# Four directly multiplied tiles of an up-projection: another place for one result half, two more PSUM banks, and a later point in each slot for low parts and eviction adds

## The chip, the cores and the metric

One Trainium2 chip, and one of its cores. The metric is the device time of one execution in microseconds (us), the median of several runs. Engines are named as the profile names them: PE (TensorE), DVE (VectorE), ACT (ScalarE), POOL (GpSimd) and SP, whose queue issues the DMAs of this stage.

## The reference

One decoder layer on x of 1 x 1024 x 1024: three attention and convolution branches behind one input projection, one output projection, and a gated MLP with a causal convolution. The change lies where the output projection ends and the MLP begins:

```python
x = x + jnp.einsum('bsd,de->bse', y, w_o[l])
h2 = rmsnorm(x, ln2_g[l])
u = jnp.einsum('bsd,df->bsf', h2, w_up[l])                # 1024 -> 2 * 2816
u = causal_dwconv(u, ffn_conv_w[l], ffn_conv_b[l])        # 3 taps along s
hidden = jax.nn.silu(u[..., :D_FF]) * u[..., D_FF:]
x = x + jnp.einsum('bsf,fd->bsd', hidden, w_down[l])
```

Everything is float32; the kernel must come close to that.

## The kernel before

Everything is kept transposed: features on the 128 partitions, the 1024 positions along the free axis in two halves of 512. A float32 product is made of three float32r matmuls (`mm3`): weight high part by input high part, by input low part, and weight low part by input high part. A weight block of 128 x 512 is loaded by SP, ACT casts it to its high part (`whs`, L856), and POOL or DVE subtracts to get the low part (`wls`, L857): that is `wsplit`.

The up-projection has 22 tiles j, each with a gate half and a value half of 128 features. Tiles 4 to 20 are made by a scheme with seven products for each tile (`pipeline`, banks `mA`, `m`). It needs sums and differences of the input's quarters, which don't exist yet when the MLP begins. So the first four tiles are multiplied directly, in `spread`, while those are being made. `spread` is a list of 40 slots, each of 12 matmuls on one weight block: slots 0 to 7 ("o") are the second half of the output projection, slots 8 to 39 are (j, i, q): tile j, positions half i, and q = 0 to 3 for gate and value (q % 2) with the input's first or second 512 features (q // 2).

Names of the input quarters: b11 and b21 are the first positions half (first and second 512 features), b12 and b22 the second, and t1 = b12 - b11. In half i = 0, q < 2 multiplies b11 into banks p0 and p1 of the tile, and q = 2, 3 multiplies b21 into p2 and p3; the result is p2 + p0 (gate) and p3 + p1 (value). In half i = 1, q < 2 adds the product of t1 onto what p0 and p1 still hold, which makes it that of b12, and q = 2, 3 adds that of b22. So those matmuls may only start when the first half's eviction has read p0 and p1. An eviction (`slot_evict`) is an ACT copy of one bank into `ur` and, for i = 0, a DVE add of the other.

The order on DVE, ACT and POOL is the order in which `spread` calls them: for slot s the matmuls, the eviction of slot s - 1, the split of the weights of slot s + 3, then `work`, which takes jobs from `jobs_` by a budget of units: `scaled` and `comb_split` make b, t1, t2, t3, t4 (a DVE operation, an ACT cast for the high part, and a DVE subtraction for the low part one call later), and `conv_value`, `conv_gate`, `conv_end` are the causal convolution of finished tiles (an ACT operation, two DVE taps of 1023 and 1022 columns, Silu on ACT, a DVE product of 1024). PE's own order is made by a scheduler. The evictions in `LATE` (slots 15, 34, 35) are put off: that of slot 15 because the tile `rb`, into which the value half of j = 1 goes, still holds a norm, and those of 34 and 35 because both `ur` buffers still hold tile 2 until its convolution is done.

Ahead of `spread`, `out(e, 1, 0)` makes a first part of the output projection's second half, with two PSUM buffers of tag "mm" (`mm_ps`); `pt_ps` is a tag with five.

Of the kernel before, what the change touches and what calls it, by code (L numbers as in the profile page):

```python
# [8 lines left out]
F32 = mybir.dt.float32  # L9
# [51 lines left out]
def hybrid_trunk(ctx: ExitStack, tc: tile.TileContext, xT, par, win, wvf, wo, wup, wdn,  # L61
# [96 lines left out]
    with ExitStack() as cb_:  # L158
# [19 lines left out]
        def mm_ps(name):  # L178
            return ps1.tile([P, HALF], F32, tag="mm", name=name, bufs=2)
# [455 lines left out]
        def out(e, i, part):  # L635

            if part == 0:
                if e % 2 == 0:
                    xh_[i].append(pair_tile(f"x1_{i}_{e}", [P, 2, HALF], F32))
                nc.sync.dma_start(X(e, i), xT[e][:, HS[i]])  # L640
            w = load_w(wo[e][:, 4 * part:4 * part + 4], 4, f"wo{e}_{i}_{part}")
            ps = mm_ps(f"oc{e}_{i}_{part}")
            yield from mm_gen(ps, w, y_part(part, i), slice(0, HALF))
            V.tensor_add(X(e, i), ps, X(e, i))

# [131 lines left out]
    def ur_tile(name, shape=None):  # L777
        return fp.tile(shape or [P, S], F32, tag="ur", name=name, bufs=2)
# [68 lines left out]

    wcount = [0]

    def wsplit(j, n, t, nk=4, eng=G):  # L850
        with tc.high_priority():
            wcount[0] += 1
            pool, tag, b = (fp, "x", 1) if wcount[0] % 4 == 0 else (wp, "", 3)
            hi = pool.tile([P, 4, P], F32R, tag=f"{tag}wh", name=f"wh{j}_{n}", bufs=b)[:, 0:nk]
            lo = pool.tile([P, 4, P], F32R, tag=f"{tag}wl", name=f"wl{j}_{n}", bufs=b)[:, 0:nk]
            A.copy(hi, t)  # L856
            eng.tensor_sub(lo, t, hi.bitcast(F32))  # L857
        return [(hi[:, k, :], lo[:, k, :]) for k in range(nk)]

    def prod(ps, n, w, x=None, first=True, **kw):  # L860
# [280 lines left out]

    HT = ((0, 0), (1, 0), (0, 1), (1, 1), (2, 0), (2, 1), (3, 0), (3, 1))
    slots = [("o", e, 0) for e in range(DT)] + [(j, i, q) for j, i in HT for q in range(4)]
    pro = pipeline(NFF - 1)

    LATE = [slots.index(s) for s in ((1, 0, 3), (3, 0, 2), (3, 0, 3))]
    raws, ws_, ps_, gone = {}, {}, {}, set()
    acc2 = r2b[:, HS[1]]
    g1 = [half_pair(f"g1_{k}", "c") for k in range(4)]
# [7 lines left out]
        nc.sync.dma_start(raws[s], src)  # L1157

    def slot_prep(s):
        ws_[s] = wsplit("s", s, raws.pop(s), eng=G if s < 11 else V)  # L1160

    def slot_mm(s):
        j, i, q = slots[s]
        w = ws_.pop(s)
        if j == "o":
            ps_[s] = bank(f"o{i}")
            prod(ps_[s], 0, w, x=y_last)
        elif i == 0:
            ps_[j, q] = bank(f"p{j}_{q}")
            prod(ps_[j, q], 1 if q < 2 else 2, w, skip_group_check=True)  # L1170
        else:
            prod(ps_[j, q % 2], 5 if q < 2 else 3, w, first=False, skip_group_check=True)

    def slot_evict(s):

        j, i, q = slots[s]
        gone.add(s)
        if j == "o":
            x = X(i, 1)
            V.tensor_add(x, ps_[s], x)  # L1180
            A.activation(acc2 if i == 0 else r2vt[:, 1] if i == DT - 1 else sq2[:, i % 2], x, AF.Square)
            return 1
        if q < 2:
            return 0
        if (i, q) == (0, 2):
            ur[j] = [cp.tile([P, S], F32, tag=t, name=f"ur{j}{t}", bufs=1) for t in ("rb2", "rb")] if j == 1 else                 [ur_tile(f"ur{j}_{c}") for c in range(2)]
        u = ur[j][q - 2][:, HS[i]]
        if i == 0:
            A.copy(u, ps_[j, q])
            V.tensor_add(u, ps_[j, q - 2], u)  # L1190
            return 1
        A.copy(u, ps_[j, q - 2])
        return 0
# [4 lines left out]
    def jobs_():  # L1198

        for r, b in enumerate((b11, b21)):  # L1200
            for k in range(4):
                def f(r=r, b=b, k=k):
                    scaled(b[k], 4 * r + k, 0)
                    comb_split(("b11", "b21")[r], k, b[k])
                yield 0, 2, f

        def norm():
            ps = bank("r2ps1")
            colsum(ps, acc2, r2vt[:, 1, :])
            rsqrt(r2b[:, HS[1]], ps, D, r2vt[:, 0, :], r2vt[:, 1, :])  # L1210
        yield 9, 4, norm
        yield 0, 1, comb_low
        for k in range(4):
            def f(k=k):
                scaled(b12[k], k, 1)
                V.tensor_sub(b12[k], b12[k], b11[k])
                comb_split("t1", k, b12[k])
            yield 0, 3, f
        for k in range(4):
            def f(k=k):  # L1220
                scaled(b22[k], 4 + k, 1)
                if k == 3:
                    slot_evict(LATE[0])
                comb_split("b22", k, b22[k])
            yield 0 if k < 3 else LATE[0] + 1, 2, f

        def combos(k):
            V.tensor_sub(b22[k], b22[k], b12[k])
            comb_split("t2", k, b22[k])
            yield 2  # L1230
            V.tensor_sub(b11[k], b22[k], b11[k])
            comb_split("t3", k, b11[k])
            yield 2
            V.tensor_sub(b21[k], b22[k], b21[k])
            comb_split("t4", k, b21[k])
            yield 2

        def conv_value(j):
            gated[j] = [None, cv_tile(j)]
            conv_first(j, ur[j][1], gated[j][1], 1)  # L1240
            yield 0
            for d in (1, 2):
                conv_tap(j, ur[j][1], gated[j][1], 1, d)
                yield 2

        def conv_gate(j):
            cg = gated[j][0] = x_tile(f"cg{j}").rearrange("p i s -> p (i s)")
            conv_first(j, ur[j][0], cg, 0)
            yield 0
            for d in (1, 2):  # L1250
                conv_tap(j, ur[j][0], cg, 0, d)
                yield 2
            A.activation(cg, cg, AF.Silu)
            yield 0

        def conv_end(j):
            comb_low()
            cg, cv = gated[j]
            V.tensor_mul(cv, cv, cg)
            tail[j] = store(j)  # L1260
            yield 2

        def turns(*gens):
            gens = list(gens)
            while gens:
                for g in list(gens):
                    u = next(g, None)
                    if u is None:
                        gens.remove(g)
                    else:  # L1270
                        yield u

        def stored(j):
            for f in tail[j]:
                f()
                yield 2

        def late():
            for s in LATE[1:]:
                slot_evict(s)  # L1280
                yield 1


        for first, gens in ((0, [combos(0)]), (0, [combos(1)]), (21, [conv_value(0), combos(2)]),
                            (0, [conv_gate(0), combos(3)]), (24, [conv_value(1), conv_end(0)]),
                            (24, [conv_gate(1)]), (25, [conv_end(1)]), (0, [stored(1)]), (32, [conv_value(2)]),
                            (32, [conv_gate(2)]), (34, [conv_end(2)]), (35, [late()]), (35, [pro_steps()])):
            gen = turns(*gens)
            while True:
                got = []  # L1290
                def f(gen=gen, got=got):
                    got.append(next(gen, None))
                    return got[0]
                yield first, None, f
                if got[0] is None:
                    break
# [6 lines left out]
    def spread():  # L1303
# [4 lines left out]
        for s in range(FRONT):  # L1308
            slot_prep(s)
            slot_load(s + FRONT)  # L1310
        units = 0

        def work(units):
# [6 lines left out]

        for s in range(len(slots)):
            units = min(units, 2) + 4
            if slots[s][0] == 3 and slots[s][1]:
                while LATE[-1] not in gone:
                    work(1)
            slot_mm(s)
            if s and s - 1 not in LATE:
                units -= slot_evict(s - 1)
            if 3 <= s < 2 + DT - 1:
                V.tensor_add(acc2, acc2, sq2[:, (s - 2) % 2])  # L1330
                units -= 1
            n = s + FRONT
            if n < len(slots):
                slot_prep(n)
                units -= n >= 11
                if n + FRONT < len(slots):
                    slot_load(n + FRONT)
            else:
                units = work(99)
                assert job is None  # L1340
                next(pro)
            units = work(units)
        assert job is None
        slot_evict(len(slots) - 1)
        after(FIRST - 1, 0)
        drain(pro)

# [169 lines left out]
```

## Time and profile before

| | |
|---|---|
| time of 3 runs, median (lowest to highest) | 1292.29 us (1291.47 to 1294.94) |
| the profiled execution | 1292.03 us, of it 1290.2 us from first to last instruction |
| PE busy | 1212.5 us, 94% |
| DVE, ACT, POOL busy | 1004.1, 635.1, 452.5 us |
| granted TensorE clock, mean | 0.979 of full speed |

All times below are from the start of that span. Each matmul row on PE gives 0.39 us, since matmuls overlap; at full clock they start 0.227 us apart, so a slot of 12 takes 2.72 us. Idle time of DVE, ACT and POOL only matters where PE waits for its end.

### The profile page before, as it was taken

The page shows a single profiled execution, that of the slowest core. Times are in us where ns is not written, and L with a number is a line of the kernel's source. Part 1 is how long each engine was busy: PE and PEld are TensorE (multiplying, and loading weights), DVE is VectorE, ACT ScalarE, POOL GpSimd, SP SyncE. Part 2 cuts the span into 40 slices and gives each one's busy share as a digit, 9 for nine tenths or more (in the row PEclk, how much of TensorE's full clock was granted, in tenths as well). Part 3 has the DMA queues.
Part 4 walks back from the last instruction along what each step waited for, and adds up shares of the span by engine and source line. Part 5 has one row for each costly group of instructions (what it writes and reads, how often), then busy time and mean ns, then how long its engine had stood idle before and what let it go on. Part 6 is the DMA issues. An engine that isn't in the chain of part 4 may idle for free.

```text
span 1290.2 us, 17279 instructions
## 1 busy us (share of the span) xinstructions
PE 1212.5 (94%) x6061; PEld 986.0 (76%) x6061; DVE 1004.1 (78%) x1521; ACT 635.1 (49%) x1158; POOL 452.5 (35%) x361
## 2 busy tenths in 40 slices
PE   7999899999999998999988999999999989999996
PEld 5897577777777876777666888888888868786795
DVE  8799886654565577777786888888888898979756
ACT  6422365564556475544564554554544564443233
POOL 4575122322242141341001121111112476867754
PEclk9899799999999999999998999999999989999998
DMA  6102021111001233232231332332233364634203
GB/s 221 42 17 68 23 67 33 58 58 58 25 26 42 76 106 115 71 125 82 82 131 58 106 116 105 106 121 69 98 122 118 128 192 150 195 109 141 74 24 131
DMA packets 64758, 118.93 MB, mean 92 GB/s; under 512 B 6800, under 2 KB 26784, under 8 KB 64672
## 3 DMA queue, kind: packets, MB, share of 16 engines
q1 hardware_dynamic: 64096, 117.57, 27.5%
q8 instruction: 47, 0.77, 0.3%
q14 instruction: 39, 0.32, 0.1%
q10 hardware_dynamic: 576, 0.28, 0.1%
HBM read 93.89 MB, written 23.93 MB: 91 GB/s over the span
## 4 chain that ended last, share of the span: by engine, by line
PE 48%; DVE 7%; issue 3%; ACT 2%; POOL 2%; DMA 1%; DVEq 0%; SPq 0%; POOLq 0%; ACTq 0%
PE mA L116 5%; PE mA L117 5%; PE mA L118 5%; PE m L116 4%; PE m L118 4%; PE m L117 4%; PE d L118 3%; PE d L117 3%; PE d L116 3%; POOL wld L857 1%; PE oc L116 1%; PE oc L117 1%; PE oc L118 1%; PE dl L117 1%; PE dl L116 1%
## 5 line engine op out<-in xcount | busy, mean ns | idle before, releaser
L857 POOL TENSOR_TENSOR wl<-a,wh 128x512 fp32r<-128x512 f32 x38 | 51.2, 1349 | 277.2 <-ACT wh L856 275.1
L453 DVE TENSOR_TENSOR pl<-pt,ph 128x512 fp32r<-128x512 f32 (+1 forms) x120 | 75.3, 635 | 59.3 <-ACT ph L452 56.2
L118 PE MATMUL d<-hc,wld 128*128 128x512 f32 x252 | 100.8, 401 | 8.2 <-POOL wld L857 8.0
L117 PE MATMUL d<-hc,whd 128*128 128x512 f32 x252 | 99.8, 396 | 1.9 <-DVE hc L1132 1.9
L116 PE MATMUL d<-hc,whd 128*128 128x512 f32 x252 | 99.5, 396 | 0.8 <-ACT hc L1131 0.4
L418 ACT ACTIVATE w<-w,mn 128x128 f32<-128x128 f32 (+7 forms) x96 | 73.8, 770 | 49.5 <-DVE mn L412 49.1
L273 DVE SCALAR_TENSOR_TENSOR yc<-gv,prm,yc 128x1023 f32<-128x1023 f32 (+29 forms) x60 | 86.1, 1435 | 0.9
L452 ACT CAST ph<-pt 128x512 fp32r<-128x512 f32 (+1 forms) x120 | 63.5, 538 | 41.1 <-PE pt L448 30.1
L463 PE MATMUL av<-ph,VS 128*128 128x256 f32 x240 | 64.6, 288 | 10.6 <-ACT ph L452 6.8
L448 PE MATMUL pt<-idf,w 128*128 128x128 f32 x432 | 69.7, 280 | 4.2 <-ACT w L418 3.4
L857 POOL TENSOR_TENSOR wld<-a_d,whd 128x384 fp32r<-128x384 f32 x48 | 61.0, 1275 | 16.2 <-ACT whd L856 13.4
L118 PEld LDWEIGHTS d<-hc,wld 128*128 128x128 f32 x252 | 48.1, 191 | 23.4 <-POOL wld L857 13.7
L856 ACT CAST wh<-a 128x512 fp32r<-128x512 f32 x72 | 44.8, 622 | 38.4 <-issue 23.7
L857 DVE TENSOR_TENSOR wl<-s,wh 128x512 fp32r<-128x512 f32 x51 | 40.9, 802 | 28.4 <-ACT wh L856 28.4
L464 PE MATMUL av<-pl,VS 128*128 128x256 f32 x240 | 62.0, 291 | 0.9 <-DVE pl L453 0.9
L463 PEld LDWEIGHTS av<-ph,VS 128*128 128x128 f32 x240 | 45.8, 191 | 21.6 <-ACT ph L452 10.4
L448 PEld LDWEIGHTS pt<-idf,w 128*128 128x128 f32 x432 | 50.1, 142 | 12.1 <-ACT w L418 5.0
L116 PE MATMUL m<-t,wh 128*128 128x512 f32 x152 | 59.1, 389 | 0.0
L117 PE MATMUL m<-t,wh 128*128 128x512 f32 x152 | 59.1, 389 | 0.0
L118 PE MATMUL m<-t,wl 128*128 128x512 f32 x152 | 59.1, 389 | 0.0
L117 PEld LDWEIGHTS d<-hc,whd 128*128 128x128 f32 x252 | 47.9, 190 | 12.7 <-DVE hc L1132 2.7
L103 POOL TENSOR_TENSOR wl_wo<-raw_wo,wh_wo 128x512 fp32r<-128x512 f32 x24 | 32.2, 1344 | 72.1 <-ACT wh_wo L102 65.5
(418 smaller groups left out, 3965.0 us busy)
## 6 DMA issues: line engine op xcount, KB each, us to landing
a<-in_wup SPq DMA_DIRECT2D x72, 256.0 KB, 2.5
tr<-td SPq DMA_DIRECT2D x27, 512.0 KB, 5.0
a_d<-in_wdn SPq DMA_DIRECT2D x48, 192.0 KB, 2.4
d<-in_wup SPq DMA_DIRECT2D x32, 256.0 KB, 2.5
raw_wo<-in_wo SPq DMA_DIRECT2D x24, 256.0 KB, 2.6
td<-cv SPq DMA_DIRECT2D x9, 512.0 KB, 2.8
td<-ta SPq DMA_DIRECT2D x9, 512.0 KB, 3.8
td<-tb SPq DMA_DIRECT2D x9, 512.0 KB
```

The source lines that it names most:

```text
L116: T.matmul(ps, lhsT=wh, rhs=xh[:, sl], start=first, stop=False, **kw)
L117: T.matmul(ps, lhsT=wh, rhs=xl[:, sl], start=False, stop=False, **kw)
L118: T.matmul(ps, lhsT=wl, rhs=xh[:, sl], start=False, stop=last, **kw)
L273: V.scalar_tensor_tensor(y[:, d:], u[:, 0:S - d], col(wc + 30 - d), y[:, d:], op0=ALU.mult, op1=ALU.add)
L418: A.activation(w[:, 0:nk], w[:, 0:nk], AF.Exp, scale=-1.0, bias=mn[h], accum_out=den[qi // 4][:, 4 * h + qi % 4:4 * h + qi % 4 + 1])
L448: T.transpose(pt[:, P * b:P * b + P], ws[2 * i + j, h][:, P * kt:P * kt + P], idf)
L452: A.copy(ph[:, 0:w], pt[:, 0:w])
L453: V.tensor_sub(pl[:, 0:w], pt[:, 0:w], ph[:, 0:w].bitcast(F32))
L463: T.matmul(o, lhsT=vt, rhs=phl[0][:, r], start=kt == 0, stop=False)
L464: T.matmul(o, lhsT=vt, rhs=phl[1][:, r], start=False, stop=kt == 2 * i + 1)
L856: A.copy(hi, t)
L857: eng.tensor_sub(lo, t, hi.bitcast(F32))
```

## The change

It does five things. (1) The value half of tile 1 goes into a buffer of tag "cb" of the MLP's pool and not into `rb`, so the eviction of slot 15 is no longer put off, and `combos(3)` (t2, t3, t4 of the last chunk) moves behind the first tile's convolution. (2) Slots 18 to 21 change places in pairs: t1 products of tiles 0 and 1 come first, then the b22 products. (3) The t1 products of tile 3 start new banks p4 and p5; its second half is evicted as copy and add, two adds more on DVE. (4) Low parts of the weights and eviction adds are put in a list `later` and issued at the end of the slot, behind `work`. (5) `out(e, 1, 0)` takes its banks from the tag with five buffers.

```diff
-            ps = mm_ps(f"oc{e}_{i}_{part}")
+            ps = (pt_ps if i else mm_ps)(f"oc{e}_{i}_{part}")
...
-    def wsplit(j, n, t, nk=4, eng=G):
+    def wsplit(j, n, t, nk=4, eng=G, later=None):
...
             A.copy(hi, t)
-            eng.tensor_sub(lo, t, hi.bitcast(F32))
+            f = lambda: eng.tensor_sub(lo, t, hi.bitcast(F32))
+            if later is None:
+                f()
+            else:
+                later.append(f)
...
+    slots[18:22] = slots[20:22] + slots[18:20]
     pro = pipeline(NFF - 1)
 
-    LATE = [slots.index(s) for s in ((1, 0, 3), (3, 0, 2), (3, 0, 3))]
+    LATE = [slots.index(s) for s in ((3, 0, 2), (3, 0, 3))]
+    later = []
...
-            prod(ps_[j, q % 2], 5 if q < 2 else 3, w, first=False, skip_group_check=True)
+            if j == 3 and q < 2:
+                ps_[j, q + 4] = bank(f"p{j}_{q + 4}")
+            prod(ps_[j, q % 2 + (4 if j == 3 else 0)], 5 if q < 2 else 3, w,
+                 first=j == 3 and q < 2, skip_group_check=True)
...
-            ur[j] = [cp.tile([P, S], F32, tag=t, name=f"ur{j}{t}", bufs=1) for t in ("rb2", "rb")] if j == 1 else                 [ur_tile(f"ur{j}_{c}") for c in range(2)]
+            ur[j] = [ur_tile(f"ur{j}_{c}") for c in range(2)] if j != 1 else \
+                [cp.tile([P, S], F32, tag="rb2", name="ur1g", bufs=1), cb_tile("ur1v", [P, S])]
...
-        if i == 0:
-            A.copy(u, ps_[j, q])
-            V.tensor_add(u, ps_[j, q - 2], u)
+        if i == 0 or j == 3:
+            A.copy(u, ps_[j, q + 2 * i])
+            later.append(lambda: V.tensor_add(u, ps_[j, q - 2], u))
...
-                            (0, [conv_gate(0), combos(3)]), (24, [conv_value(1), conv_end(0)]),
+                            (0, [conv_gate(0)]), (24, [conv_value(1), conv_end(0)]), (0, [combos(3)]),
...
-            if slots[s][0] == 3 and slots[s][1]:
-                while LATE[-1] not in gone:
-                    work(1)
             slot_mm(s)
...
             units = work(units)
+            while later:
+                later.pop(0)()
```

On DVE, where the weights of slots 14 and 15 are split (names: g1 is the buffer in which b12 and b22 are made, ur0 the result of tile 0), before:

```order
L1190 TENSOR_TENSOR ur0_0_6099<-p0_0_6012,ur0_0_6099 128x512
L857 TENSOR_TENSOR wls_14_6104<-d14_6032,whs_14_6103 128x512
L1196 SCALAR_TENSOR_TENSOR g1_1_5781<-x1_1_0_5571,prm_67,r2b_4765 128x512
L1216 TENSOR_TENSOR g1_1_5781<-g1_1_5781,tb1_5762 128x512
L815 TENSOR_TENSOR t1_0_6084<-g1_0_5780,t1_0_6084 128x512
L1190 TENSOR_TENSOR ur0_1_6100<-p0_1_6034,ur0_1_6100 128x512
L857 TENSOR_TENSOR wls_15_6130<-d15_6051,whs_15_6129 128x512
```

and of the change:

```order
L1206 SCALAR_TENSOR_TENSOR g1_1_5781<-x1_1_0_5571,prm_67,r2b_4765 128x512
L1226 TENSOR_TENSOR g1_1_5781<-g1_1_5781,tb1_5762 128x512
L815 TENSOR_TENSOR t1_0_6083<-g1_0_5780,t1_0_6083 128x512
L1200 TENSOR_TENSOR ur0_0_6099<-p0_0_6012,ur0_0_6099 128x512
L857 TENSOR_TENSOR wls_14_6103<-d14_6031,whs_14_6102 128x512
```

The add and the low part, which stood ahead of the three job instructions of their slot, stand behind them.

On DVE around the adds that free the banks of slots 28 and 29 (tile 2's p0 and p1; cv and cg are the convolutions of value and gate, tb3 and g1_3 the sources of t2, t3, t4 of the last chunk), before:

```order
L924 SCALAR_TENSOR_TENSOR cg0_6450<-ur0_0_6099,prm_67,cg0_6450 128x1023
L857 TENSOR_TENSOR wls_29_6471<-d29_6400,whs_29_6470 128x512
L1231 TENSOR_TENSOR tb3_5764<-g1_3_5783,tb3_5764 128x512
L815 TENSOR_TENSOR t2_3_6453<-g1_3_5783,t2_3_6453 128x512
L1190 TENSOR_TENSOR ur2_0_6493<-p2_0_6407,ur2_0_6493 128x512
```

and of the change:

```order
L928 SCALAR_TENSOR_TENSOR cg0_6449<-ur0_0_6099,prm_67,cg0_6449 128x1023
L857 TENSOR_TENSOR wls_28_6445<-d28_6373,whs_28_6444 128x512
L928 SCALAR_TENSOR_TENSOR cg0_6449<-ur0_0_6099,prm_67,cg0_6449 128x1022
L815 TENSOR_TENSOR t4_2_6427<-tb2_5763,t4_2_6427 128x512
L1267 TENSOR_TENSOR cv0_6375<-cv0_6375,cg0_6449 128x1024
L857 TENSOR_TENSOR wls_29_6467<-d29_6399,whs_29_6466 128x512
L928 SCALAR_TENSOR_TENSOR cv1_6473<-ur1v_6201,prm_67,cv1_6473 128x1023
L1200 TENSOR_TENSOR ur2_0_6491<-p2_0_6406,ur2_0_6491 128x512
```

Tile 0's convolution now ends ahead of that add, the last chunk's t2, t3, t4 come behind it, and one tap of tile 1 has moved ahead of it too.

On ACT at the Silu of that convolution, with what each instruction waits for, of the change:

```order
L856 CAST whs_29_6466<-d29_6399 128x512 [waits DMAHW4_49,PE_49,Activation_49]
L1261 ACT_TABLE_LOAD [waits DVE_49]
L1261 ACTIVATE cg0_6449<-cg0_6449 128x1024 [waits Activation_49]
L924 ACTIVATE cv1_6473<-ur1v_6201,prm_67 128x1024 [waits DVE_49]
L1199 COPY ur2_0_6491<-p2_2_6453 128x512 [waits PE_49]
```

Before, the load of the table (`L1253 ACT_TABLE_LOAD`) had no wait and stood behind the copies of ur2; now it waits for DVE (the second tap of cg0), and the copy of ur2_0 stands behind it.

On PE the first matmul of slot 36, which read t1 into tile 3's p0 and waited for DVE, now starts bank p4, and what it waits for is its own weights.

## Rows read from the trace of the kernel before

**Rows 1.** Stretches: us; busy PE, PEld, DVE, ACT, POOL; PE clock; DMA share, GB/s

```profile
564.28:586.04 21.76, 21.76 (x97) 18.02 (x96) 20.38 (x26) 12.60 (x23) 11.22 (x8) 1.00 0.29 97
598.85:652.42 53.57, 45.91 (x194) 35.04 (x192) 42.46 (x65) 27.17 (x47) 0.00 (x0) 1.00 0.26 84
...
695.55:1000.00 304.45, 304.45 (x1345) 252.10 (x1344) 264.36 (x312) 154.64 (x225) 51.66 (x40) 1.00 0.30 105
```

**Rows 2.** What PE waited for, whole run: us, times, longest

```profile
PE p L116 <- DVE ur L1190: 11.8, 2, 7.1
PE d L118 <- POOL wld L857: 8.0, 10, 1.9
...
PE oc L116 <- DVE x L644: 3.7, 3, 1.8
...
PE p L117 <- DVE b L815: 1.5, 2, 1.0
```

**Rows 3.** PE in order of time: start, us, instruction, [idle before]

```profile
598.85 0.39 PE L116 MATMUL p<-b,whs 128*128 128x512 f32 x1
...
652.42 0.79 PE L116 MATMUL p<-t,whs 128*128 128x512 f32 x1 [4.75 <-DVE ur L1190]
...
656.73 0.39 PE L116 MATMUL p<-t,whs 128*128 128x512 f32 x1
...
683.03 0.79 PE L116 MATMUL p<-t,whs 128*128 128x512 f32 x1 [7.07 <-DVE ur L1190]
...
695.55 0.39 PE L116 MATMUL mA<-b,wh 128*128 128x512 f32 x1
```

**Rows 4.** DVE from 596.85 to 652.42, grouped: busy, mean ns | idle before

```profile
L857 DVE TENSOR_TENSOR wls<-d,whs 128x512 fp32r<-128x512 f32 x18 | 12.4, 688 | 7.5 <-ACT whs L856 7.5
...
L1190 DVE TENSOR_TENSOR ur<-p,ur 128x512 f32<-128x512 f32 x3 | 2.1, 692 | 2.3 <-ACT ur L1189 2.3
...
L1190 DVE TENSOR_TENSOR ur1rb<-p,ur1rb 128x512 f32<-128x512 f32 x2 | 1.4, 692 | 1.2 <-ACT ur1rb L1189 1.2
```

**Rows 5.** DVE in order of time

```profile
596.85 0.68 DVE L815 TENSOR_TENSOR b<-tb,b 128x512 fp32r<-128x512 f32 x1
...
608.44 0.69 DVE L857 TENSOR_TENSOR wls<-d,whs 128x512 fp32r<-128x512 f32 x1 [0.61 <-ACT whs L856]
609.05 0.74 DVE L1196 SCALAR_TENSOR_TENSOR g<-x,prm,r2b 128x512 f32<-128x512 f32 x1
609.83 0.69 DVE L1216 TENSOR_TENSOR g<-g,tb 128x512 f32<-128x512 f32 x1
...
642.52 1.28 DVE L924 SCALAR_TENSOR_TENSOR cv<-ur,prm,cv 128x1022 f32<-128x1022 f32 x1
643.71 0.69 DVE L857 TENSOR_TENSOR wls<-d,whs 128x512 fp32r<-128x512 f32 x1
...
651.67 0.69 DVE L1190 TENSOR_TENSOR ur<-p,ur 128x512 f32<-128x512 f32 x1 [0.57 <-ACT ur L1189]
```

**Rows 6.** ACT in order of time

```profile
658.03 1.28 ACT L1253 ACT_TABLE_LOAD   x1
659.32 1.06 ACT L1253 ACTIVATE cg<-cg 128x1024 f32<-128x1024 f32 x1
660.29 1.23 ACT L920 ACTIVATE cv<-ur1rb,prm 128x1024 f32<-128x1024 f32 x1
...
699.17 0.56 ACT L1039 COPY u<-mA 128x512 f32<-128x512 f32 x1
```

**Rows 7.** PE in order of time, ahead of the slots

```profile
545.11 1.10 PE L136 MATMUL r2ps<-r2b,onf 128*128 128x512 f32 x2 [0.53 <-DVE r2b L700]
...
548.36 0.39 PE L118 MATMUL oc<-y,wl_wo 128*128 128x512 f32 x1
550.59 0.47 PE L116 MATMUL oc<-y,wh_wo 128*128 128x512 f32 x1 [1.84 <-DVE x L644]
...
551.13 0.39 PE L118 MATMUL oc<-y,wl_wo 128*128 128x512 f32 x1
```

More of the change, by code (lines that the diff above doesn't have):

```diff
@@ L1159, in slot_prep @@
     def slot_prep(s):
-        ws_[s] = wsplit("s", s, raws.pop(s), eng=G if s < 11 else V)
+        ws_[s] = wsplit("s", s, raws.pop(s), eng=G if s < 11 else V, later=later)
     def slot_mm(s):
@@ L1221, in f @@
                 scaled(b22[k], 4 + k, 1)
-                if k == 3:
-                    slot_evict(LATE[0])
                 comb_split("b22", k, b22[k])
-            yield 0 if k < 3 else LATE[0] + 1, 2, f
+            yield 0, 2, f
         def combos(k):
@@ L1278, in late @@
         def late():
-            for s in LATE[1:]:
+            for s in LATE:
                 slot_evict(s)
@@ L1342, in spread @@
             units = work(units)
+            while later:
+                later.pop(0)()
         assert job is None
         slot_evict(len(slots) - 1)
+        later.pop(0)()
         after(FIRST - 1, 0)
```

## The prediction

> **What bounds the kernel now.** I read the stretches first, since PE's busy share of the whole run hides stages with different limits. From 695.55 on PE is busy all of 304.45 us at full clock, and in slots 0 to 7, from 564.28 to 586.04, all of 21.76 us, which is 2.72 us a slot; the slots between are not like that [rows 1]. Then the list of PE's waits over the run: its longest entry is two waits of 11.8 us together for the DVE add of an eviction, and it lies in this stage [rows 2]. In order of time these are the first matmuls of slot 28 (652.42) and of slot 36 (683.03): both multiply t1 into a bank that the eviction of the half before hasn't read yet [rows 3]. From slot 12 (598.85) to the first matmul behind the slots (695.55) lie 96.70 us, where 28 slots need 76.2: 20.5 us too much. The reader is to see that DVE is what is late. Up to slot 28 it is busy 42.46 of 53.57 us and stands idle 11.0 us for ScalarE: 7.5 ahead of a weight's low part, 3.5 ahead of eviction adds [rows 1, 4]. Each such wait is some 0.6 us: the cast of the slot's weights, or the copy, has only just begun when DVE comes to the instruction that needs it, and the work behind can't pass [rows 5]. As PE is full behind this stage, what is saved here should reach the end.
>
> **What each part costs.** First a check that DVE's queue can be counted. Narrow operations (512 columns) start 0.605 us apart, wide ones (1022 to 1024) 1.2, and one that reads the result just ahead of it takes 0.17 more [rows 5]. Before, from 596.85 to the add that frees slot 28, stand 63 narrow and three wide ones and four such pairs: 38.1 + 3.6 + 0.7 = 42.4. With the 11.0 of 15 waits, and 0.085 for each of them (a wait also ends the overlap of 0.69 and 0.605), it comes to 651.5; the row says 651.67. That will do.
>
> Low parts and adds at a slot's end (4). Each cast now has three or four job instructions as its cover, and in the new order I find no wait of DVE for ScalarE until tile 0's convolution; without that cover the 0.6 us would be back in each slot. What is late instead is the low part, some 1.8 us within its own slot. Counting from 596.85 (slot 12's part now stands behind the norm and ends at 598.1), slot 13's ends at 600.1, slot 14's at 603.3, slot 15's at 606.5. PE needs them at its third matmul, 0.45 behind the slots' starts at 601.57, 604.29 and 607.01: margins of 1.9, 1.4 and 1.0 us (1.2 at slot 12), and more from slot 16 on. So this costs nothing.
>
> Slot order and tile 1's place (1, 2). The b22 products begin at slot 20 (620.6) and no longer at 18. The last low part of b22 ends at 618.9 by the count, so PE's waits for b, 1.5 us, and what followed from them are gone [rows 2]. The adds that free slots 18 and 19 end at 612.8 and 615.2, and those slots start at 615.2 and 617.9: 2.4 us of cover.
>
> The add for slot 28 (1, 4). From 596.85 to it now stand 61 narrow and six wide operations and four pairs: 36.9 + 7.2 + 0.7 = 44.8. Three wide ones are moved in, the rest of tile 0's convolution and a tap of tile 1. Three waits for ScalarE remain. The first tap of cv0 needs the copy of slot 21's bank (filled at 626.05), behind a cast of t4, then a cast and a 1.23 us activation [rows 6]: ready at 629.1, where DVE is there at 628.4, 0.75. The first tap of cg0 stands behind a cast of t4 that needs DVE's own last result, a cast and an activation: 1.25. The product of cv0 and Silu(cg0) needs the table load, which now waits for the second tap (640.1), 1.28, and then 1.06: ready at 642.5, where DVE is there at 640.6, 1.9. So 596.85 + 44.8 + 3.9 = 645.5, and the add ends at 646.1. Slot 28 could start at 598.85 + 16 x 2.72 = 642.4. PE still waits 3.7 us, but starts 6.3 us earlier than at 652.42.
>
> At this place a page speaks against the change. The one table load of the stage takes 1.28 us, and its Silu starts 0.01 behind its end [rows 6]. The Trainium skill, ScalarE: Activation LUTs, section What ACT_TABLE_LOAD costs, gives 1283 ns for the load and about 1380 ns of drain with it. By the page the add would end 1.4 us later than by the row, and the sum would be 1276.7. The row agrees with the first figure and shows nothing of the second; I go by the row.
>
> What that wait costs in clock. After the wait of 4.75 us slot 28 took 4.31 us (652.42 to 656.73) and not 2.72, 1.6 lost, as its first matmuls ran at half the clock [rows 3]. After a wait of 1.84 us nothing of that kind is seen: two matmuls in 0.54 us [rows 7]. 3.7 is nearer the first: 1.6, with 0 as the other end.
>
> Slots 28 to 36 (3). Before, 30.61 us from 652.42 to 683.03 [rows 3]; now 8 x 2.72 + 1.6 = 23.4: 7.2 saved. Slot 36's bank is the eighth behind tile 2's p0, which slot 30's eviction empties some five slots earlier. The late evictions of tile 3 still wait for tile 2's convolution: from the start of slot 35 a cast 0.6, an activation 1.25, four taps and two low parts 6.2, Silu 1.06 and the two copies 1.05 make 10.1 us of the five slots' 13.6. Then the cast (0.6) and POOL's low part (1.3) for the first matmul behind the slots end 1.6 us ahead of it. So nobody waits there now; without that cover the 7.07 us would be back in part.
>
> Slots 36 to 39: before 12.52 us (683.03 to 695.55), at the lower clock again; now 10.9: 1.6 saved [rows 3].
>
> The two adds more of tile 3 (3), 1.2 us of DVE. They stand between ScalarE's copies of p4 and p5 and its activation of tile 3's values, and behind that on ScalarE is the copy u of `mA`, for which the second product into `mA` waits. Before, that copy ended at 699.73, 1.26 us ahead of that matmul, which stands 2 x 2.72 behind 695.55 [rows 3, 6]. By the count it ends 0.15 us too late: 0.2 lost, from 0 to 2.
>
> The banks of `out(e, 1, 0)` (5). The wait of 1.84 us ended by L644 is for a DVE add that stands behind the norms of the branches. With five banks nothing asks for it. The matmul at 548.36 is followed 2.23 us later, not 0.23: 2.0 saved, less 0.2 for a matmul that now stands behind the norm's column sum, which waits for DVE at 545.11 in any case [rows 7]. The weights ahead are ready: 1.8, with 0 as the other end.
>
> Sum: 6.3 + 7.2 + 1.6 - 0.2 + 1.8 = 16.7. The profiled execution took 1292.03, 0.3 under the median: 1275.3 us.
>
> **The rivals.** (A) DVE keeps up, and slot 28 doesn't wait. For it: DVE's waits there come from the order of a few instructions, and 3.9 us of them would do. Against it: three wide operations and the table load stand ahead of the add. It gives the 3.7 and the 1.6 as well: 1270.
>
> (B) The wait moves on: the copy u comes 2 us late behind tile 3's adds, and the clock falls once more (1.6): 1278.7. With slot 28's wait as long as before (4.75) it is 1279.8. For it: the count leaves no margin there. Against it: DVE has 0.6 us waits of its own to lose.
>
> (C) Changing the table costs as much again as its row, 1.28: slot 28 starts at 647.4, the time is 1276.6. Against it: the Silu 0.01 behind the load [rows 6]. The page named above says something of the kind.
>
> (D) The gain is given back later: PE, earlier at the seven-product tiles, finds DVE behind. For it: DVE is busy 264.36 of 304.45 us there, and the down projection already waits 8.0 us for POOL [rows 1, 2]. Against it: nothing there hangs on a fixed time, transfers follow the buffers that PE frees, and by the count DVE is 1.5 us later relative to PE than before. The time would stay, about 1291.
>
> (E) Slower: low parts at the slot's end come too late, and PE waits at the third matmul of slot after slot. DVE's 97 operations up to the end of tile 2's convolution take 68.3 of the 76.2 us without waits, so 7.9 are free. With before's 20.5 it is slower as soon as DVE waits over 28.4 us in the stage, 1 us a slot, where it was 11.0 in 16 slots. At 1.25 us a slot, 35 in all, it ends at 1292.0 + 35 - 7.9 - 20.5 - 1.8 = 1296.8. For it: margins of only 1.0 to 1.9 us at slots 12 to 15.
>
> **How the numbers follow.** The sum has 0.62, A 0.13, B 0.12, C 0.03, D 0.06, E 0.04. The likeliest gives 1275.3. The range goes from half a us under A, 1269.5, to B with the 1.8 of the banks lost, 1281.5; D and E, 0.10, stay out. About 0.3% (4 us) is what a measurement of this kernel can tell from none: faster are the sum, A, B and C, 0.90; D is the same, 0.06; E slower, 0.04.
>
> **What would show it.** Right: one wait of PE for tile 2's add at slot 28, 2 to 5 us, and none at slot 36; DVE's idle time ahead of low parts up to slot 28 down from 7.5 to under 2; 81 to 82 us from slot 12 to the first `mA`; no wait at the fourth `oc`. Wrong: PE waiting for `wls`, for the copy u or for tile 1's adds; DVE idle ahead of its adds as before; a first `mA` that comes 17 us earlier and an end that doesn't.

## The result, and the profile after

| | before | after |
|---|---|---|
| median (lowest to highest), 6 runs each | 1294.11 us (1291.47 to 1297.97) | 1280.37 us (1275.48 to 1281.69) |
| ratio, 95% interval | | 0.9875 (0.9859 to 0.9892) |
| the profiled execution | 1292.03 us | 1275.48 us |

The change makes the kernel faster by 1.25%, some 14 to 16 us; 16.7 were forecast. The profiled execution, 1275.48, lies right at the forecast 1275.3, but that is partly luck. It reaches the norm ahead of the slots (545.11 in [rows 7]) at 538.98, 6.1 us earlier than before, and all of that is there 290 us further ahead already (one of ScalarE's table loads, at 251.54 and before at 257.82), where nothing is changed. A second profile of the same kernel reaches the norm at 545.46 and takes 1279.73. So I compare stages and not ends. The median, 1280.37, lies inside the range of 1269.5 to 1281.5, but near its slow end.

The changed kernel by stretches (us; busy PE, PEld, DVE, ACT, POOL; PE clock; DMA share, GB/s): from slot 12 to 1 us ahead of slot 28, then the first `mA` to its second product, and the rest of the seven-product tiles.

```profile
590.86:637.06 46.20, 43.68 (x193) 35.85 (x191) 42.66 (x64) 30.06 (x50) 0.00 (x0) 1.00 0.33 102
...
672.49:680.93 8.44, 6.91 (x30) 5.10 (x28) 6.87 (x10) 4.37 (x6) 0.12 (x1) 1.00 0.31 106
680.93:1000.00 319.07, 319.07 (x1409) 264.20 (x1408) 278.89 (x329) 161.14 (x238) 59.10 (x44) 1.00 0.31 106
```

What its PE waited for over the run (us, times, longest):

```profile
PE d L118 <- POOL wld L857: 9.2, 10, 2.1
...
PE p L116 <- DVE ur L1200: 3.6, 1, 3.6
...
PE oc L116 <- DVE x L644: 1.9, 2, 1.4
```

Of the 11.8 us for eviction adds [rows 2] one wait of 3.6 is left; the fourth `oc` no longer waits. Where it is, by PE in order of time (slots 12, 28, 29, 36, the first `mA`, and what follows it):

```profile
590.86 0.39 PE L116 MATMUL p<-b,whs 128*128 128x512 f32 x1
...
638.10 0.50 PE L116 MATMUL p<-t,whs 128*128 128x512 f32 x1 [3.56 <-DVE ur L1200]
...
642.55 0.39 PE L116 MATMUL p<-t,whs 128*128 128x512 f32 x1
...
661.61 0.39 PE L116 MATMUL p<-t,whs 128*128 128x512 f32 x1
...
672.49 0.39 PE L116 MATMUL mA<-b,wh 128*128 128x512 f32 x1
...
678.95 0.50 PE L116 MATMUL m<-t,wh 128*128 128x512 f32 x1 [0.85 <-ACT wh L856]
...
680.36 0.50 PE L118 MATMUL m<-t,wl 128*128 128x512 f32 x1 [0.68 <-DVE wl L857]
...
680.93 0.39 PE L116 MATMUL mA<-t,wh 128*128 128x512 f32 x1
```

Read against [rows 3]: slot 28 starts 47.24 us behind slot 12 (53.57 before), slot 29 another 4.45 later, slot 36 runs without a stop, and the first `mA` comes 81.63 behind slot 12 (96.70). Behind it there is a loss that wasn't there before: the second product of `mA` starts 8.44 behind the first, where 5.44 is the work that stood between the two before (two products of 2.72).

DVE up to slot 28, grouped (busy, mean ns | idle before):

```profile
L857 DVE TENSOR_TENSOR wls<-d,whs 128x512 fp32r<-128x512 f32 x19 | 13.0, 683 | 0.0
...
L928 DVE SCALAR_TENSOR_TENSOR cg<-ur,prm,cg 128x1023 f32<-128x1023 f32 (+1 forms) x2 | 2.6, 1280 | 1.2 <-ACT cg L924 1.2
L928 DVE SCALAR_TENSOR_TENSOR cv<-ur,prm,cv 128x1023 f32<-128x1023 f32 (+1 forms) x2 | 2.6, 1278 | 0.4 <-ACT cv L924 0.4
...
L1267 DVE TENSOR_TENSOR cv<-cv,cg 128x1024 f32<-128x1024 f32 x1 | 1.2, 1224 | 1.9 <-ACT cg L1261 1.9
```

The 11.0 us of idle time [rows 4] are 3.5 now, at the three places that were named. ACT in order of time, the table load:

```profile
632.03 1.28 ACT L1261 ACT_TABLE_LOAD   x1 [2.46 <-DVE cg L928]
633.33 1.06 ACT L1261 ACTIVATE cg<-cg 128x1024 f32<-128x1024 f32 x1
```

It waits for DVE's second tap, and the Silu starts 0.02 us behind its end. The Trainium skill (ScalarE: Activation LUTs, What ACT_TABLE_LOAD costs) puts a drain of about 1380 ns there; as in [rows 6], none is seen.

Last, the new loss. DVE, then POOL, then ACT, in order of time around the first `mA`:

```profile
669.07 0.68 DVE L1022 TENSOR_TENSOR s<-a,a 128x512 f32<-128x512 f32 x1
669.78 1.67 DVE L1025 TENSOR_TENSOR s<-s,a 128x512 f32<-128x512 f32 x1
671.38 1.78 DVE L1027 TENSOR_TENSOR a<-a,a 128x512 f32<-128x512 f32 x1
673.42 0.69 DVE L1030 TENSOR_TENSOR s<-a,s 128x512 f32<-128x512 f32 x1 [0.26 <-DMA a<-in_wup]
674.03 1.28 DVE L1200 TENSOR_TENSOR ur<-p,ur 128x512 f32<-128x512 f32 x2
...
675.83 1.28 DVE L1200 TENSOR_TENSOR ur<-p,ur 128x512 f32<-128x512 f32 x2
```

```profile
669.50 3.11 POOL L857 TENSOR_TENSOR wl<-a,wh 128x512 fp32r<-128x512 f32 x2 [8.75 <-ACT wh L856]
```

```profile
677.15 1.24 ACT L924 ACTIVATE cv<-ur,prm 128x1024 f32<-128x1024 f32 x1 [3.87 <-DVE ur L1200]
678.29 0.60 ACT L856 CAST wh<-a 128x512 fp32r<-128x512 f32 x1
678.80 1.24 ACT L924 ACTIVATE cg<-ur,prm 128x1024 f32<-128x1024 f32 x1
679.95 0.56 ACT L1043 COPY u<-mA 128x512 f32<-128x512 f32 x1
```

Tile 3's four late adds stand on DVE behind four sums of weights. Two of these take 1.67 and 1.78 us while POOL makes two low parts, the fourth waits for a transfer. The adds end at 677.1; ACT's activation of tile 3 waits for them, and behind it stand the cast of the next weights and the copy u, which ends at 680.5 where the second product was due at 677.93. PE fills a part of that time: four matmuls of the product behind it now stand ahead of it in its order. They wait for their own cast (0.85 us) and low part (0.68), and these are PE's only stops here: no row shows it waiting for the copy u, which is done 0.4 us ahead of the second product. Cast and copy hang on the same activation.

### The profile page after: what moved, and what is told of

Same layout as the page of the kernel before. It is cut to its first block, busy times and chain, and to the rows that moved or that the text cites. A ratio compares the mean times of both kernels' runs of the same rounds, so it can differ in the third digit from the quotient of the medians.

```text
span 1273.7 us, 17279 instructions
## 1 busy us (share of the span) xinstructions
PE 1203.4 (94%) x6061; PEld 980.2 (77%) x6061; DVE 1007.5 (79%) x1523; ACT 634.7 (50%) x1158; POOL 450.9 (35%) x361
## 4 chain that ended last, share of the span: by engine, by line
PE 51%; DVE 4%; POOL 3%; issue 3%; DMA 1%; ACT 1%; DVEq 0%; POOLq 0%; ACTq 0%
PE mA L116 5%; PE mA L117 5%; PE mA L118 5%; PE m L118 4%; PE m L116 4%; PE m L117 4%; PE d L118 3%; PE d L117 3%; PE d L116 3%; PE p L116 2%; PE p L117 2%; PE p L118 2%; POOL wld L857 2%; PE oc L116 1%; PE oc L117 1%
## 5 line engine op out<-in xcount | busy, mean ns | idle before, releaser
L117 PEld LDWEIGHTS d<-hc,whd 128*128 128x128 f32 x252 | 48.0, 191 | 14.6 <-DVE hc L1136 3.7
L116 PEld LDWEIGHTS d<-hc,whd 128*128 128x128 f32 x252 | 48.2, 191 | 13.9 <-ACT whd L856 2.7
L1385 DVE TENSOR_TENSOR x<-d,x 128x512 f32<-128x512 f32 x84 | 54.7, 679 | 3.2 <-PE d L118 2.7
```

Of the source, the lines that this page charges most:

```text
L116: T.matmul(ps, lhsT=wh, rhs=xh[:, sl], start=first, stop=False, **kw)
L117: T.matmul(ps, lhsT=wh, rhs=xl[:, sl], start=False, stop=False, **kw)
L1385: V.tensor_add(c, ps, c)
```

## The experiments

Stages are read from PE in order of time in each kernel's profile; ratios go against the kernel before on the same chip (its medians there: 1295.3 to 1296.4 us). "Slot 12 to `mA`" would be 76.2 without a stop, "`mA` to `d`" (first `mA` to the first down product) is 342.72 without one.

| kernel | slot 12 to `mA` | `mA` to its 2nd product | `mA` to `d` | median us (runs) | ratio to before, interval |
|---|---|---|---|---|---|
| before | 96.70 | 5.44 | 342.72 | 1294.11 (6) | |
| before_again | 96.97 | 5.44 | 342.72 | 1292.74 (1) | |
| after | 81.63 | 8.44 | 344.83 | 1280.37 (6) | 0.9875, 0.9859 to 0.9892 |
| after_again | 81.57 | 8.09 | 344.50 | 1279.73 (1) | |
| banks_alone | 89.21 | 10.19 | 347.19 | 1290.59 (10) | 0.9966, 0.9947 to 0.9984 |
| low_alone | 85.99 | 5.45 | 342.73 | 1286.68 (6) | 0.9925, 0.9896 to 0.9954 |
| banks_undone | 79.42 | 15.68 | 352.96 | 1286.61 (6) | 0.9928, 0.9902 to 0.9954 |
| banks_undone2 | 92.73 | 5.44 | 342.72 | 1285.67 (7) | 0.994, 0.9923 to 0.9958 |
| later_undone | 91.55 | 10.30 | 346.72 | 1292.73 (10) | 0.999, 0.9975 to 1.0006 |
| adds_now | 81.11 | 9.94 | 347.95 | 1282.25 (4) | 0.9892, 0.9857 to 0.9927 |
| pool_off | 81.62 | 9.14 | 345.54 | 1281.29 (4) | 0.9894, 0.9866 to 0.9922 |
| tail_conv | 81.65 | 5.44 | 342.72 | 1276.20 (4) | 0.9866, 0.9832 to 0.9901 |
| own2 | 76.18 | 11.02 | 348.61 | 1277.41 (4) | 0.9849, 0.9811 to 0.9887 |
| own2_tail | 76.18 | 6.09 | 344.35 | 1273.19 (4) | 0.9826, 0.9798 to 0.9854 |

**Both kernels once more.** 

> The changed kernel once more, for a second profile. In its first profile PE reaches the column sum of the second norm 6.1 us earlier than in the kernel before, though nothing ahead of it is changed, and loses 2.1 us behind the slots and 4.4 us in the down projection. Theory: the 6.1 and the 4.4 differ from execution to execution (clock, and who meets whom), the stage between doesn't. Then slot 12 to the first mA is 81.6 within 0.3, the wait at slot 28 is 3.6, the loss behind the first mA is 2.1 again, and the time up to slot 12 or that behind the slots differs by several us. Rival: the 4.4 is the change's own, the gain given back: then the down projection takes 195.3 us again (1017.3 to 1212.6) against 190.9 before.

 

> The kernel before once more, for a second profile. Theory: slot 12 to the first mA is 96.7 within 0.5, with waits of 4.7 and 7.1 at slots 28 and 36 and 1.84 at the fourth oc; ahead of the norm and in the down projection (190.9 us in the first profile) it may differ by several us. Rival (the 4.4 us are the change's): 190.9 within 0.5 again.

 The stage comes back within 0.3 us on both sides, the wait at slot 28 is 3.56 again, the loss behind the first `mA` 1.8 (344.50 against 342.72). Ahead of the slots and in the down projection the same kernel differs: the norm lies at 538.98 and 545.46, the down projection takes 195.51 and 193.65; before 191.09 and 192.78. All other kernels here show 192.5 to 195.7. So of the 4.4 us that the first profile loses there, 2.6 are left when both profiles of each kernel are averaged (194.6 against 191.9); the next section comes back to it.

**The banks of tile 3 alone, on the kernel before.**

```diff
+            if j == 3 and q < 2:
+                ps_[j, q + 4] = bank(f"p{j}_{q + 4}")
...
-            if slots[s][0] == 3 and slots[s][1]:
-                while LATE[-1] not in gone:
-                    work(1)
```

> The kernel before with one part of the change alone: tile 3's t1 products in banks of their own, two adds more, no forced drain. My account of the change: slot 36's stop goes (7.2 with the 0.4 of clock between, and 1.6 of slots 36 to 39), slot 28 keeps its 4.7 and slot 29 its low clock, and the copy u or the casts behind the slots come up to 2 us late: 6.5 to 8.8 us less than before. Rival: without the low parts at the slot's end DVE is too late for the end of the stage, the wait only moves behind the slots, and under 4 us are gained.

 The stop at slot 36 goes: 89.21, 7.6 less. But 4.5 of it come back behind the slots (347.19), and the time falls by 0.34%, 4.4 us. My account gave 6.5 to 8.8, the rival under 4: the size lies between, with an interval (2 to 7 us) that reaches into both, and the place where it is lost is the rival's. DVE's fourth sum waits 2.63 us for its transfer there, and tile 3's adds stand behind it.

**The low parts alone, on the kernel before.**

```diff
-            eng.tensor_sub(lo, t, hi.bitcast(F32))
+            f = lambda: eng.tensor_sub(lo, t, hi.bitcast(F32))
...
+                later.append(f)
...
+            while later:
+                later.pop(0)()
```

> The kernel before with one part of the change alone: the low parts of the weights at the slot's end (adds at once, order of the slots and banks as before). My account: DVE's 7.5 us of idle time ahead of low parts go, the add for slot 28 comes some 7 us earlier, so PE's stop there (4.75) and slot 28's low clock (1.6) go; the stop at slot 36 stays at 6.5 to 7.5, since what it waits for hangs on PE's own slots 30 and 31 and the convolution behind them. Slot 12 to the first mA falls from 96.7 to 90 to 91, and the time by 5 to 7. With the 4.7 of the banks alone that would leave 2 to 4 of the whole for the rest. Rival: the parts need one another; alone the wait only moves on, to slot 36 or behind the slots, and under 3 us are gained.

 More than expected: 85.99, 10.8 less, and 0.75% in time. Slot 28 doesn't wait at all; the one stop left in the slots is the old one at slot 36:

```profile
675.60 0.80 PE L116 MATMUL p<-t,whs 128*128 128x512 f32 x1 [7.68 <-DVE ur L1195]
```

So moving one subtraction within its slot is worth more than the rest of the change adds to it. PE's two waits for b [rows 2], which the prediction took away by the new slot order, are gone here without it. It also points at what the new order of the jobs costs, which no run took apart: here tile 2's add stands ahead of tile 0's product and of tile 1's first tap, and is in time; in the full change it stands behind them, and 3.56 us of waiting and 1.7 of low clock at slot 28 are back.

**Without the banks.** The first of two kernels let tile 3's late adds slip behind its t1 products, which therefore ran without waiting for them: its tile 3 is wrong, and it answers nothing about the wait. 

> The changed kernel without tile 3's own banks (with the forced drain at slot 36 again). My account: the add that frees slot 36 stands behind tile 2's convolution product, which ends at 669.1 where slot 36 starts at 661.6, so PE stops there for 8 to 9 us, runs the four slots at the low clock (1.6), and the 2.1 us behind the slots are gone: 7 to 9 us slower than the changed kernel. Rival: DVE, earlier by the other parts, has tile 2's convolution done sooner once nothing of tile 3 stands between: 3 us or less.

 The second has the adds in their place.

```diff
-            prod(ps_[j, q % 2 + (4 if j == 3 else 0)], 5 if q < 2 else 3, w,
-                 first=j == 3 and q < 2, skip_group_check=True)
+            prod(ps_[j, q % 2], 5 if q < 2 else 3, w, first=False, skip_group_check=True)
...
+                while LATE[-1] not in gone:
+                    work(1)
+                while later:
+                    later.pop(0)()
```

> The changed kernel without tile 3's own banks, now with the late adds of tile 3's first half really ahead of its t1 products (in the run before this one they had slipped behind them, so that kernel's result for tile 3 was wrong and nothing waited at slot 36). My account: those adds stand behind tile 2's convolution product, which ended 7.5 us behind the start of slot 36 in the changed kernel; PE stops there 8 to 9 us, the four slots run at the low clock (1.6), and the loss of 2 us behind the slots is gone: slot 12 to the first mA 91 to 92.5 instead of 81.6, the time 7 to 9 us above the changed kernel. Rival: nothing of tile 3 stands in DVE's way now, the convolution is done sooner: 3 us or less.

 Nearly as my account said: 92.73 from slot 12, 11.1 more, and nothing lost behind the slots. The time is 5.3 us above the changed kernel by the medians and 8.4 by the ratios, where 7 to 9 were expected. The stop (7.55 at slot 36, 8 to 9 expected) is not shorter than before for DVE's having caught up:

```profile
673.63 0.80 PE L116 MATMUL p<-t,whs 128*128 128x512 f32 x1 [7.55 <-DVE ur L1197]
```

**Without the list `later`, and without it for the adds alone.**

```diff
-        ws_[s] = wsplit("s", s, raws.pop(s), eng=G if s < 11 else V, later=later)
+        ws_[s] = wsplit("s", s, raws.pop(s), eng=G if s < 11 else V)
...
-            later.append(lambda: V.tensor_add(u, ps_[j, q - 2], u))
+            V.tensor_add(u, ps_[j, q - 2], u)
```

> The changed kernel with low parts and eviction adds issued at once again, all else kept. My account: DVE meets ScalarE's casts and copies half done again, 0.6 us each, 10 to 11 us up to the add that frees slot 28; PE's wait there, 3.6 now, becomes 12 to 14 and slot 12 to the first mA 91 to 94: 9 to 12 us slower. Rival: what counts is the order of the slots and the banks, DVE's waits only fill time in which it would wait for PE or ScalarE anyway: 3 us or less.

 Nearly all of the gain is gone, 0.999 of the time before. DVE up to slot 28, grouped, and PE at slot 28:

```profile
L857 DVE TENSOR_TENSOR wls<-d,whs 128x512 fp32r<-128x512 f32 x18 | 12.4, 688 | 7.5 <-ACT whs L856 7.5
```

```profile
652.35 0.80 PE L116 MATMUL p<-t,whs 128*128 128x512 f32 x1 [9.42 <-DVE ur L1200]
```

The 7.5 us ahead of low parts are back to the tenth [rows 4]. PE's wait is shorter than expected (9.42, not 12 to 14), and 4.0 us more are lost behind the slots (346.72). 

> The changed kernel with the eviction adds issued at once and only the low parts at the slot's end. It splits the last part of the change in two. By the rows of before the adds' waits for ScalarE are 0.7 us each: four or five of them ahead of slot 28 make DVE 2.5 to 3.5 later; tile 2's add itself comes ahead of a tap of 1.2. So slot 28's wait grows from 3.6 by 1 to 2.5, and the low parts account for the rest of the 10 us that both together are worth. Rival: the copies are long done where the adds stand, since DVE is behind ScalarE: no change, or 1.2 less.

 The rival is right: slot 28's wait is 3.15 and not 4.6 to 6.1, since with the low parts out of the way DVE comes to the adds when the copies are done (0.6 us idle ahead of five adds, in place of 3.5 [rows 4]). DVE, grouped, up to slot 28, and its fourth sum behind the slots:

```profile
L1200 DVE TENSOR_TENSOR ur<-p,ur 128x512 f32<-128x512 f32 x3 | 2.1, 689 | 0.6 <-ACT ur L1199 0.6
...
L1200 DVE TENSOR_TENSOR ur1v<-p,ur1v 128x512 f32<-128x512 f32 x1 | 0.7, 692 | 0.0
L1200 DVE TENSOR_TENSOR ur1g<-p,ur1g 128x512 f32<-128x512 f32 x1 | 0.7, 690 | 0.0
```

```profile
683.81 0.69 DVE L1030 TENSOR_TENSOR s<-a,s 128x512 f32<-128x512 f32 x1 [2.47 <-DMA a<-in_wup]
```

Behind the slots, though, this kernel loses 5.2 us (347.95): DVE's fourth sum waits 2.47 us for its transfer, with two adds of tile 3 behind it. That transfer is issued at the first `mA`, where it was 2.9 us ahead of it in the changed kernel. In the three kernels with such a wait (this one, banks_alone and later_undone) it is issued 0.03 us behind the end of POOL's first two low parts (here 680.21 behind 680.18), in the changed kernel 0.1 us behind their start. That suggests a buffer that POOL still reads; no run shows it. The deferred adds are worth something there, not at slot 28 as I had counted.

**The loss behind the first `mA`.** Two edits to the changed kernel: the low parts of the first two weights on DVE and not on POOL, and the first convolution steps of tile 3 a product later.

```diff
-                hl[g] = wsplit(j, n, raw[j, SRC[n]], eng=G if (g - FRONT) % NP in (4, 5) else V)
+                hl[g] = wsplit(j, n, raw[j, SRC[n]], eng=G if g >= FRONT and (g - FRONT) % NP in (4, 5) else V)
```

```diff
                 if k < 4:
-                    after(j - 1, k + 1)
+                    for m in (k + 1,) if j > FIRST or k > 1 else (0, 1, 2) if k else ():
+                        after(j - 1, m)
...
-        after(FIRST - 1, 0)
```

> The changed kernel with the low parts of the first two weights behind the slots on DVE and not on POOL. In the changed kernel's profile two DVE sums of weights take 1.67 and 1.78 us, not 0.69, while POOL makes these two low parts (3.11 for both). Theory: the two engines get in each other's way; then the sums take 0.69 each, DVE saves 2.1 and pays 1.2 for the low parts, and the copy u ends 0.9 us earlier: of the 2 us behind the slots about 1 is left. Rival: the sums are slow for their transfers or of themselves: they stay at 1.7, DVE is 1.2 later, and the loss grows to 3.

 DVE in order of time in that kernel:

```profile
677.70 0.69 DVE L1025 TENSOR_TENSOR s<-s,a 128x512 f32<-128x512 f32 x1
678.31 0.68 DVE L1027 TENSOR_TENSOR a<-a,a 128x512 f32<-128x512 f32 x1
680.83 0.69 DVE L1030 TENSOR_TENSOR s<-a,s 128x512 f32<-128x512 f32 x1 [1.83 <-DMA a<-in_wup]
681.44 0.69 DVE L857 TENSOR_TENSOR wl<-a,wh 128x512 fp32r<-128x512 f32 x1
682.04 1.28 DVE L1200 TENSOR_TENSOR ur<-p,ur 128x512 f32<-128x512 f32 x2
683.24 0.68 DVE L857 TENSOR_TENSOR wl<-a,wh 128x512 fp32r<-128x512 f32 x1
...
684.44 1.28 DVE L1200 TENSOR_TENSOR ur<-p,ur 128x512 f32<-128x512 f32 x2
```

The mechanism of the theory holds, its price doesn't. Without POOL beside them the two sums take 0.69 and 0.68, so POOL was what made them slow; but then the fourth sum waits 1.83 us for its weights. It starts 0.43 us behind the first `mA` (680.40), in the changed kernel 0.93: of the 2.1 us saved 0.5 come through. The two low parts on DVE cost 1.2, so the adds end 0.7 later (5.32 us behind the first `mA`, 4.62 before), and the loss grows from 2.0 to 2.8.

> The changed kernel with the first convolution steps of tile 3 issued one product later, so that on ScalarE the copy u and the casts of the next weights stand ahead of its two activations, which wait for DVE's adds. Theory (the 2 us behind the slots are the copy u, queued behind an activation that waits for tile 3's late adds): first mA to second product of mA goes from 8.1 to 8.4 back to 5.44 and to the first down product from 344.7 to 342.7, 2.0 us gained. Rival: DVE itself is too late there, its low parts or m's evictions come next: no gain.

 As the theory says: the second product comes 5.44 behind the first, nothing is lost (342.72). ACT in order of time, then the second product on PE:

```profile
677.47 0.63 ACT L856 CAST wh<-a 128x512 fp32r<-128x512 f32 x1
679.69 0.59 ACT L1043 COPY u<-mA 128x512 f32<-128x512 f32 x1 [1.59 <-PE mA L118]
...
681.17 1.24 ACT L924 ACTIVATE cv<-ur,prm 128x1024 f32<-128x1024 f32 x1 [0.38 <-DVE ur L1201]
```

```profile
682.21 0.39 PE L116 MATMUL mA<-t,wh 128*128 128x512 f32 x1
```

The copy u ends at 680.28, 1.9 us ahead of that product, and the activations stand behind it. The cast has moved ahead of them too, so this kernel shows that the activations were in the way, not which of the two behind them held PE. The median is 4 us below the changed kernel, by the ratios it is 1.2, and the intervals overlap: the gain is read from the rows, the times alone don't show it.

**Tile 2's banks too.** On the changed kernel, then together with the edit just shown.

```diff
-            if j == 3 and q < 2:
+            if j >= 2 and q < 2:
...
-        if i == 0 or j == 3:
+        if i == 0 or j >= 2:
```

> The changed kernel with t1 products in banks of their own for tile 2 too (two adds more on DVE). Theory (DVE's order, not its total, holds PE at slot 28, and what comes earlier there runs into the copy u behind the slots): slot 28's wait (3.6) and its slow clock (1.7) go, the first mA comes 5 us earlier after slot 12 (76.2 to 77), but the second product of mA, held by DVE's adds and the transfer of the weights that they stand behind, hardly earlier: 8.1 to 8.4 there becomes 11 to 14, and the time falls by 0 to 2. Rival A: the loss behind the slots stays at 3, all 5 us are gained. Rival B: two adds more make DVE late for low parts before that, and PE stops in the slots.

 No stop is left in the slots: 76.18. Alone, most of the 5.4 us is lost again behind the slots (348.61, 3.9 more than in the changed kernel), as the theory has it; 1.5 are left. 

> The same, with the first convolution steps of tile 3 one product later as in the kernel with that edit alone. Theory: the copy u no longer stands behind the activations that wait for tile 3's adds, so most of the 5 us come through: slot 12 to the first mA 76.2 to 77, the second product of mA 5.4 to 8 behind it, the time 5 to 7 below the changed kernel. Rival: DVE is the bound by its total there, and low parts or adds come too late by what was saved: 2 us or less below.

 Together 5.7 come through against the changed kernel, 5.4 in the slots and 0.3 behind, and all that PE waited for from 550 to 1000 in this kernel are two short waits:

```profile
PE mA L116 <- ACT u L1043: 0.7, 1, 0.7
PE mA L118 <- POOL wl L857: 0.4, 1, 0.4
```

At 1273.19 us this is the fastest kernel here, 0.9826 of before, 7 us below the changed one by the medians and 6.3 by the ratios. DVE's total isn't what bounds the slots.

## Why the prediction came out as it did

**Slot 28, 6.3 us: right.** It starts 47.24 us behind slot 12; 47.25 were counted (646.1 against 598.85). The wait is 3.56 for 3.7, the low clock behind it 4.45 - 2.72 = 1.7 for 1.6. DVE's three waits for ScalarE are 0.42, 1.15 and 1.86, where 0.75, 1.25 and 1.9 stood. The three waits are 0.5 us shorter in sum, and the 0.085 for each wait, which the count of before had in, was left out here: that the total fits to 0.01 is partly luck. Still, counting a queue by spacings from the trace held here within 0.5 us over 49 us and 67 instructions.

**Who earns it: partly wrong.** I gave the 11.0 us of DVE's idle time to "low parts and adds at a slot's end" together. At slot 28 the low parts alone earn it: low_alone has 10.8 of the stage's 15.2 us, adds_now is no later at slot 28 than the full change. That the adds' 3.5 would go by themselves once the low parts are late had escaped me.

**Slots 28 to 36 and 36 to 39, 7.2 and 1.6: right together.** From slot 28 to 36 it took 23.51 (23.4 forecast), from there to `mA` 10.88 (10.9). Without the banks the stop is back at 7.55.

**Low parts late, at no cost: right.** In the slots PE has one wait and that is for the add; rival E has nothing for it.

**The banks of `out(e, 1, 0)`, 1.8: right.** From the norm's column sum (`r2ps`) to the first matmul of slot 0 it takes 17.30 in both profiles of after, 19.17 and 19.19 in those of before: 1.9.

**The copy u, 0.2 with 2 as the far end: this is the step that was wrong.** The place cost 2.1 and 1.8 us (344.83 and 344.50 against 342.72). The chain was the one named up to the activation behind tile 3's adds; its last link wasn't: PE's stops are for the cast between that activation and the copy u, and for its low part. The term was mis-sized since the adds come late. The four sums of weights ahead of them, which the prediction doesn't name, take 4.96 us up to the first add (669.07 to 674.03), where four spacings of 0.605 are 2.4. Two of them lose 2.1 us to POOL, but without POOL a transfer would keep all but 0.5 of that. Rival B named this place and gave 1278.7, nearer to the median than the sum; its second part, a lower clock, isn't there (1.00 from 672.49 on).

**The base.** The sum stands on an execution of 1292.03. The median of six runs is 1294.11. With 15.2 from the slots, 1.9 from `oc` and less 2.0 behind the slots, 15.1 in all, that gives 1279.0, against a measured 1280.37. So of the 5.1 us between 1275.3 and the median 2.1 are the base, 1.6 the sum (the copy u 1.8, less 0.2 that the other terms brought more), and 1.4 nothing that I can name. That is within the noise: by the ratio the gain is 16.2 us, with 14 to 18 as its interval.

**Rival D, the gain given back later: not seen in the times.** The profiles of the down projection suggest 2.4 us on average (191.1 and 192.8 before, 192.5 to 195.7 in the twelve others). If the changes caused that, the measured gains should fall short of the stages' sums. They don't: for the ten timed kernels (all but the first without the banks) the gain by the ratio, of 1295 us, stands 0.7 us above that sum (the columns "slot 12 to `mA`" and "`mA` to `d`", and 1.9 where the `oc` banks are in) on average, between 2.9 above and 1.9 below. Whether a microsecond is lost there stays open.

## What to carry to other kernels

Where two engines hand work to each other inside a slot, look at how far apart producer and consumer stand in the program before counting work: here one subtraction, put behind three instructions that need nothing from the other engine, took 7.5 us of waits out of a queue that looked 80% busy. A gain in one stage is only kept if the handover behind it is early too: read, in the trace of before, what the first instruction behind the stage waits for on every engine, the transfers included, and how many microseconds of margin it had. And a second profile of the same kernel costs little and tells which stages repeat (here within 0.3 us) and which don't (6 us).

## What the runs showed of the hardware that was not expected

- DVE and POOL slow each other. Sums of two SBUF tiles on DVE take 0.69 us alone, 1.67 and 1.78 beside POOL's low parts, and POOL's take 3.11 for two where one took 1.29 alone before. With the low parts off POOL the same sums take 0.69 and 0.68. The Trainium skill (SBUF — State Buffer, Who interferes with whom) says that a DVE instruction with two SBUF inputs contends with a GpSimd instruction that reads SBUF; the runs agree.
- The same wait can cost clock or not. The fourth `oc` waited 1.84 and 1.89 us in the two profiles of before, at a granted clock of 1.00 behind it; in banks_alone and low_alone it waited 1.88, and the clock fell to 0.50, the lower of the two levels, for some 3 us: 20.78 from the norm to slot 0 and not 19.18, 1.6 us. What decides it isn't in these rows. The stretch in banks_alone:

```profile
552.83:555.83 3.00, 3.00 (x8) 2.32 (x8) 2.96 (x4) 0.00 (x0) 0.62 (x1) 0.50 0.37 111
```

What was not tried: the low parts and the banks of tile 3 without the new order of slots and jobs. By low_alone's rows, 85.99 less the 7.68 of slot 36 and some 1.6 of clock, that would leave about 76.7 from slot 12 to `mA`, an estimate, without banks for tile 2. What it would lose behind the slots isn't in it; the banks alone lost 4.5 us there.
